# Stick-breaking attention summed by parts: the running product weighs differences of neighbouring values

## The chip, the cores and the metric

The kernel runs on one core of a Trainium2 chip. The metric is the time of one execution on the device in microseconds (us). Engines are named as in the profile: PE is TensorE (PEld its weight loads), DVE is VectorE, ACT is ScalarE, POOL is GpSimd, SP is SyncE, whose queue issues nearly all DMAs.

## The reference

Two layers of a decoder trunk for 2048 tokens of width 1024. The even layer norms, projects and runs two mixers side by side: stick-breaking attention with 8 heads of 128, and a diagonal complex SSM. Both are gated, then projected out and added to the input. The odd layer is chunked gated linear attention. The change is in the attention, which computes per head, with scores z = q k / sqrt(128) and only keys s before the query t:

```python
log_beta = jax.nn.log_sigmoid(z)
log_one_minus = jnp.where(causal, log_beta - z, 0.0)
rest = lax.cumsum(log_one_minus, axis=3, reverse=True) - log_one_minus
w = jnp.where(causal, jnp.exp(log_beta + rest), 0.0)
outs.append(jnp.einsum('bhts,bshd->bthd', w, vf[:, :kend]))
```

So the weight of key s is beta(s), the sigmoid of the score, times the product of 1 - beta over all keys between s and the query. With p(s) for the product of 1 - beta(j) over j from s up to the query, the weight of s is p(s+1) - p(s).

## The kernel before, in words

Products in single precision are made of three TensorE products each: every operand is split into a high part of 12 bits and the low rest, and `mm3` (lines 67 to 69) adds high x high, high x low and low x high in PSUM. A split is a ScalarE copy (the high part) and a subtraction on VectorE or GpSimd (the low part).

`attention` loops over the heads `h`, over macro tiles `m` of 512 tokens, and in these over two pairs `pr` of 128-query blocks.

- *Projections of a macro tile* (lines 704 to 733): four times, for 128 tokens each, the normed input is split (lines 711, 712), q, k and v of the head are formed together in `pp` (line 715), squares of q and k are summed (line 719), and GpSimd forms the reciprocal root (`qkms`, `qkrs`, lines 54 and 56). VectorE applies it (`qn`, line 725), TensorE transposes q and k (line 728), and they are split (lines 731, 732). v goes straight from PSUM into its high and low part `vhi`, `vlo` (lines 721, 722). The parts of k and v stay for the whole head in a pool of 5 (`at_kv`).
- *Attention of a pair* (lines 736 to 786): for key tiles `c` of 512 from `m` down to 0, and for each of the two query blocks: scores in PSUM (line 753; in the last tile a mask of -1e30 is added by a small product, line 756); 1 - beta as a sigmoid of -z on ScalarE (`om`, line 760); beta as a sigmoid of z on ScalarE (`be`, line 762); a scan on VectorE that multiplies 1 - beta from the last key to the first and starts from the scan of the key tile before (`pt`, line 764); beta times the running product on GpSimd (line 768); transposes of the result by TensorE into `w` (line 771); a split of it into `th`, `tl` (lines 773, 774). Then `av`, one PSUM bank, collects v times weights (line 782) over all key tiles. At the end the pair is gated with `zs` (line 785) and stored (line 786).

The weights of a head's projection come ahead of it (`AttnProj.load`, lines 654 to 665): eight loads into a pool of three buffers, each split by ScalarE and GpSimd (`whi`, `wlo`, lines 314 and 315) into a pool of eight, so that the next head's parts can be formed as the last projection of this head gives up buffers. In the last head `after(m)` also calls loads and splits for the output projection (lines 1264 to 1277); some of its products run within the end of attention.

Engines run their queues in order. Which instruction comes when in a queue is laid out at the build: the program is handed over in the order of the loops, and the scheduler orders the ready instructions by a simulated timeline with its own costs (`schedule_with_timeline_sim=True`, line 1343). It lets the projections of the next macro tile, and of the next head's first, run between the products of the attention.

Of the kernel before, what the change touches and what calls it, by code (L numbers as in the profile page):

```python
# [9 lines left out]
F32 = mybir.dt.float32  # L10
# [7 lines left out]
P = 128  # L18
# [31 lines left out]
def rsqrt_mean(e, pool, ss, n, dim, tag):  # L50
    """1 / sqrt(ss / dim + EPS) for a [P, n] tile of sums of squares."""
    nc = e.nc
    ms = pool.tile([P, n], F32, tag=tag + "ms", name=tag + "ms")
    nc.gpsimd.tensor_scalar(ms, ss, 1.0 / dim, EPS, ALU.mult, ALU.add)
    rs = pool.tile([P, n], F32, tag=tag + "rs", name=tag + "rs")
    nc.gpsimd.tensor_tensor(rs, ms, e.mhalf[:, :n], ALU.pow)
    return rs


def behind(e, i, first):  # L60
    """i comes behind first in their engine's queue"""
    e.tc.add_manual_dep(i.ins, first.ins.name, mybir.DependencyInfo(
        mybir.DependencyClass.NoSync, mybir.DependencyReason.DATA), reason="order")
# [8 lines left out]
class Norm:  # L72
    """hT[m][p, k, t] = rms_norm(x)[m * 512 + t, k * 128 + p], a token tile at a time"""
# [48 lines left out]
def s5_angles(e, s, lam_re, lam_im, log_dt):  # L122
    """lam, dt and sines of the angle of lam_bar and of its half; partitions and columns as in s5_setup"""
# [32 lines left out]
def s5_setup(e, room, lr, li, dt, sn, sh, b_re, b_im, c_re, c_im, dsk, bin_d, k0_d, co_d):  # L156
    """Chunk matrices of the SSM (8 tokens a chunk) into DRAM, powers of lam_bar into e.pw.

    Partition q = (parity, n) of pair i holds state n of group 2 * i + parity.
    bin_d[ri, i, (j, p), q] = lam_bar^(7-j) b_bar;  co_d[ri, i, q, (t, p)] = c lam_bar^(t+1)  # L160
    k0_d[g, (j, pi), (t, po)] = Re(c lam_bar^(t-j) b_bar) + d [t == j, pi == po]
    """
# [3 lines left out]
    # lam_bar^8, ^16, ^32, ^64: real parts, and (-im, im)  # L166
    e.pwr = [e.cst.tile([P, NI], F32, name=f"pwr{a}") for a in range(4)]
    e.pwi = [e.cst.tile([P, 2, NI], F32, name=f"pwi{a}") for a in range(4)]
    with e.pool("s5s", 1, "right") as s, e.pool("s5t", 2, "right") as s2, e.pool("s5w", 1, "right") as sw, \
# [41 lines left out]
        # powers  # L211
# [13 lines left out]
        def cmul(outs, xr, xi, yr, yi, sub, E):  # L225
            """outs[0] = xr yr + sub * xi yi, outs[1] = xr yi - sub * xi yr, x small, broadcast"""
            t = [s.tile([P, NI, 16], F32, tag=f"cm{a}", name=f"cm{a}") for a in range(4)]
            E.tensor_tensor(t[0], yr, bc(xr), MU)
            E.tensor_tensor(t[1], yi, bc(xi), MU)
            E.tensor_tensor(t[2], yi, bc(xr), MU)  # L230
            E.tensor_tensor(t[3], yr, bc(xi), MU)
            E.tensor_tensor(outs[0], t[0], t[1], SU if sub < 0 else AD)
            E.tensor_tensor(outs[1], t[2], t[3], AD if sub < 0 else SU)
# [17 lines left out]
        # G[tau] = c lam_bar^tau: real part, and minus the imaginary part  # L251
# [23 lines left out]
        # four groups at a time, on the partitions from 0, 32, 64 and 96  # L275
# [22 lines left out]
        # onto 16 partitions, then each row block of the chunk matrix  # L298
# [13 lines left out]
def split(nc, hi, lo, src, lo_eng):  # L312
    """hi + lo == src, each of 12 significant bits"""
    a = nc.scalar.activation(hi, src, AF.Copy)  # L314
    b = lo_eng.tensor_tensor(lo, src, hi.bitcast(F32), ALU.subtract)  # L315
    if TRACE is not None:
        TRACE.append(b)
    return a, b


# order in which a panel's last macro tile takes the weights: from low addresses on
# [3 lines left out]
class Panels:  # L325
    """Pools for weight panels of up to 512 columns, and for splits of hT."""
# [45 lines left out]
# token tiles to norm after these products (half, column block, row block)  # L372
# [3 lines left out]
def first_gates(e, pn, nrm, hT, w, c0, out_d, setup):  # L376
    """The first macro tile of gates(), as its tokens and weights come; returns the weights, and setup()."""
# [42 lines left out]
def gates(e, pn, hT, w, c0, out_d, row0, lo_eng, between=None, also=None, ws=None, sp=None, last=LAST):  # L420
    """out_d[row0 + f, t] = silu(h w[:, c0 + f]) for 512 columns; between(m) is called before macro tile m
    and gives the weights (the first tile is done), also(m, splits of hT) in it"""
# [3 lines left out]
    for m in range(4):  # L426
        if between is not None:
            if m == 0:
                continue
            ws = between(m)  # L430
        if m or sp is None:
            sp = pn.split(hT[m], lo_eng)
        pss = [pn.ps.tile([P, 512], F32, tag="ps", name="gps") for f in range(4)]
        # weights come, and are given up, one by one in the first and the last macro tile
        order = [(f, k) for f in range(4) for k in range(KD)]
        if m in (0, 3):
            order = [(f, k) for k in (range(KD) if m == 0 else last) for f in range(4)]
        for f, k in order:
            wh, wl = ws[k]
            hi, lo = sp[k // 2]  # L440
            c = slice(f * P, f * P + P)
            i = mm3(nc, pss[f], wh[:, c], wl[:, c], hi[:, k % 2], lo[:, k % 2], k == 0,
                    k == (last[-1] if m == 3 else KD - 1))
        if also is not None:
            also(m, sp, i)
        out = silu_out(e, pn, pss, m, out_d, row0)
# [3 lines left out]
def cplx_acc(e, tp, dst, src, lv, n, eng):  # L450
    """dst += lam^lv src for [P, 2, I, n] (re, im) views"""
# [13 lines left out]
def s5_in(e, pn, hT, w_in, bin_d, u_d, H, lo_eng):  # L465
    """u, and the states after the chunks, H[i // 8][:, ri, i % 8, 1 + c]"""
# [43 lines left out]
def scan_up(e, H, i1, tp, t2):  # L510
    """H[:, ri, i, 1 + c], of the 8 pairs from i1: contributions of chunks to the states after chunks 7, 15, .."""
# [24 lines left out]
def scan_down(e, H, i1, tp):  # L536
    """and to the states after all other chunks"""
# [11 lines left out]
def s5_out(e, H, u_d, k0_d, co_d, y_d):  # L549
    """y_d[ch, j, c] = gelu(ssm output) of token 8 * c + j"""  # L550
# [37 lines left out]
class Glu:  # L588
    """Weights, and all of the ssm output."""
# [23 lines left out]
def s5_glu(e, gl, m, zs_d, o_d):  # L613
    """o_d[1024 + f] = y sigmoid(y w_glu + b_glu) silu(z_b), features on rows, of 256 tokens"""
# [25 lines left out]
class AttnProj:  # L640
    """Pools for the projections of attention's heads."""
# [26 lines left out]
def attention(e, hT, w_in, zsT, oT, ap, w0, after):  # L668
    """oT[h * 128 + d, t]: gated attention; after(m) is called after the last head's projections"""
    nc, tc = e.nc, e.tc  # L670
    scale = float(DH) ** -0.5
    with ExitStack() as st:
# [13 lines left out]
        wk = pool("at_wk", 3)  # L686
# [5 lines left out]
        for h in range(HEADS):  # L692
            ws = w0 if h == 0 else ap.load(e, w_in, h)
            K, V = [], []
            for m in range(4):
# [7 lines left out]
                V.append((vhi, vlo))  # L703
                for half in range(2):
                    tp = tps.tile([P, 2, 256], F32, tag="tp", name="tp")
                    for tt in range(2):
# [14 lines left out]
                        nc.scalar.activation(vhi[:, i, :], ps[:, 2, :], AF.Copy)  # L721
                        nc.vector.tensor_tensor(vlo[:, i, :], ps[:, 2, :], vhi[:, i, :].bitcast(F32), ALU.subtract)
# [7 lines left out]
                    for j, (a, b) in enumerate(((qhi, qlo), (khi, klo))):  # L730
                        nc.scalar.activation(a[:, c0:c0 + 256], tp[:, j, :], AF.Copy)
                        nc.vector.tensor_tensor(b[:, c0:c0 + 256], tp[:, j, :], a[:, c0:c0 + 256].bitcast(F32),
                                                ALU.subtract)
                if h == HEADS - 1:
                    after(m)
                for pr in (2 * m, 2 * m + 1):
# [4 lines left out]
                    for c in range(m, -1, -1):  # L741
# [5 lines left out]
                        for i in range(2):  # L747
                            # keys of the pair's second block lie after all of its first block's queries
# [12 lines left out]
                            be = wk.tile([P, 512], F32, tag="be", name="be")  # L761
                            nc.scalar.activation(be[:, :n], z[:, :n], AF.Sigmoid, scale=scale)
# [5 lines left out]
                            nc.gpsimd.tensor_tensor(be[:, :n], be[:, :n], pt[:, lo + 1:513], ALU.mult)  # L768
                            w = wps.tile([P, 4, P], F32, tag="w", name="w")
                            for s in range(ni):  # L770
                                nc.tensor.transpose(w[:, s, :], be[:, s * P:(s + 1) * P], e.ident)  # L771
# [13 lines left out]
                    nc.vector.tensor_tensor(ot, av, zs, ALU.mult)  # L785
# [3 lines left out]
class OutW:  # L789
    """Operands of an output projection, the first weights on the right."""  # L790
# [6 lines left out]
    def fetch(self, room):  # L797
        """the next 4 rows of weights as they are, into a free tile of 16 KB"""
# [9 lines left out]
    def part(self, t, k4):  # L808
        """tile t of tokens, rows of weights from k4 * 512"""
# [9 lines left out]
    def queue(self, ab):  # L819
        """a pair of instructions, of ACT and DVE, comes behind another"""  # L820
# [9 lines left out]
    def load(self, ks, room=None):  # L830
        """splits rows ks, into the newest pool or a free tile of 16 KB"""
# [27 lines left out]
def out_proj(e, x, ow, dst_d, hT, g):  # L859
    """dst_d = x + o w, o_d with features on rows; with hT: rms_norm of it, transposed"""  # L860
    nc, ws, nk = e.nc, ow.ws, ow.nk
    with ExitStack() as st:
# [4 lines left out]
        # in banks that the phase before gives up first, away from those that the phase after begins with  # L867
# [17 lines left out]
        # the first two tiles together, at the pace at which weights come  # L885
# [11 lines left out]
        for t in range(NT):  # L897
            r0 = t * P
            if t == NT - 2 and hT is not None:
                # the last two tiles together, giving up weights from low addresses on  # L900
# [48 lines left out]
class Gla:  # L949
    """Gated linear attention: constants, the gate's code of every token, and weights ahead."""  # L950

    def __init__(self, e, hT, w_in, w_gate, b_gate, og):
# [6 lines left out]
        # the gate's code comes in 2 parts of 16 rows that add up; rows of high, low, high halves of  # L959
        # them go with rows of high, high, low halves of the weights  # L960
# [19 lines left out]
    def consts(self):  # L980
# [8 lines left out]
        # rows: key s, columns: query t, of two chunks of 64  # L989
# [18 lines left out]
    def code(self, m, sp, prev):  # L1008
        """rT: the code's part of high parts of weights, and its part of low ones, in halves"""
# [33 lines left out]
def gla(gl, zs_d, o_d, w0, after):  # L1043
    """o_d[f, t]: gated linear attention of normed, gated heads; after(m) is called after the last head's projections"""
# [6 lines left out]
    with ExitStack() as st:  # L1051
# [8 lines left out]
        def decays(h, m, va=None, vd=None):  # L1060
            """exp of the sums of log a in chunks, its inverse, and exp of what is left in the chunk"""
# [144 lines left out]
def tile_trunk(ctx, tc, x, even_norm_g, even_w_in, sb_q_norm_g, sb_k_norm_g, s5_lambda_re, s5_lambda_im, s5_log_dt,  # L1206
# [72 lines left out]
    attention(e, hT, w0, zs_d, o_d, ap, aw, after_head)  # L1279
# [67 lines left out]
```

## Time and profile before

| | |
|---|---|
| median of 3 runs | 2914.29 us (2914.11 to 2915.76) |
| profiled execution, first to last instruction (span) | 2920.8 us |
| PE, PEld busy | 2795.6, 2508.1 us |
| DVE, ACT, POOL busy | 1766.5, 1476.4, 1446.3 us |
| attention, about 590 to 1755 us of the span | 1165 us |
| mean granted clock of TensorE | 0.986 |

The profiled execution is one of its own. Its page gives the span and no other time; the span is 6.5 us above the median of the timed runs. Busy time of an engine is the time in which an instruction of it was running. In the rows of a group stand the line, the engine, the operation, the tile written and the tiles read, the count, then the busy time and the mean of one in ns, and behind the second bar the idle time of the engine just before these instructions with what ended it. In rows of waits stand who waited for whom, the us in total, the times, and the longest. In rows of a timeline stand the start, the duration, and the instruction; in rows of the chain, the start, the length and what ended last. Matmuls are pipelined: the rows of PE overlap one another.

### The profile page before, as it was taken

The numbers are of one execution on the slowest core, as the hardware profiler recorded it, in microseconds if no ns is written. First come the engines' busy times: TensorE is split into PE (matmuls) and PEld (weight loads), VectorE is DVE, ScalarE is ACT, GpSimd is POOL, SyncE is SP. The second block draws the span as 40 slices with busy tenths as digits, with TensorE's granted clock in tenths as the row PEclk, the third lists the DMA queues.
The fourth block names the chain that finished last, engine by engine and source line by source line (L and its number), as shares of the span: only waits on it lengthen the run. The fifth ranks groups of instructions, "written<-read, shape, count | busy, mean of one in ns | idle before, by whom it ended". The sixth has DMA issues, their size and how long they took to land.

```text
span 2920.8 us, 46867 instructions
## 1 busy us (share of the span) xinstructions
PE 2795.6 (96%) x17433; PEld 2508.1 (86%) x17433; DVE 1766.5 (60%) x2789; ACT 1476.4 (51%) x3244; POOL 1446.3 (50%) x1513
## 2 busy tenths in 40 slices
PE   7989979899999999999999989999999999999999
PEld 6788767898989898989898978888788999999887
DVE  7768965757686767676767674223344556565521
ACT  5475224556666656665656663222345556555310
POOL 7102821478787878787878752000023465555300
PEclk9999989999999999999999999999999999999999
DMA  5532136411010101010102114333131111121343
GB/s 167 153 79 79 58 103 216 142 30 33 19 33 19 33 19 33 22 34 19 33 19 65 48 44 141 105 104 93 58 101 37 37 59 55 41 73 62 115 142 112
DMA packets 217011, 207.17 MB, mean 71 GB/s; under 512 B 24528, under 2 KB 185712, under 8 KB 216272
## 3 DMA queue, kind: packets, MB, share of 16 engines
q1 hardware_dynamic: 216208, 202.08, 22.5%
q8 instruction: 138, 2.26, 0.3%
q10 hardware_dynamic: 576, 2.10, 0.2%
q14 instruction: 89, 0.73, 0.1%
HBM read 129.29 MB, written 74.58 MB: 70 GB/s over the span
## 4 chain that ended last, share of the span: by engine, by line
PE 73%; DVE 8%; POOL 8%; issue 5%; ACT 3%; DMA 3%; SPq 1%; POOLq 0%; ACTq 0%; DVEq 0%
PE av L782 5%; PE pp L68 5%; PE pp L67 5%; PE ops L68 5%; PE pp L69 5%; PE ops L67 5%; PE ops L69 5%; PE gps L67 4%; PE gps L68 3%; PE gps L69 3%; PE w L771 3%; DVE pt L764 2%; PE qk L67 2%; PE qk L69 2%; PE qk L68 2%
## 5 line engine op out<-in xcount | busy, mean ns | idle before, releaser
L768 POOL TENSOR_TENSOR be<-be,pt 128x512 f32<-128x512 f32 (+2 forms) x320 | 359.1, 1128 | 162.5 <-DVE pt L764 87.5
L712 POOL TENSOR_TENSOR sl<-hT,sh 128x1024 fp32r<-128x1024 f32 x128 | 331.6, 2591 | 65.0 <-ACT sh L711 64.0
L68 PE MATMUL pp<-wlo,sh 128*128 128x384 f32 x1024 | 353.0, 345 | 8.0 <-POOL wlo L315 8.0
L67 PE MATMUL pp<-whi,sh 128*128 128x384 f32 x1024 | 356.8, 349 | 2.3 <-ACT whi L314 2.3
L69 PE MATMUL pp<-whi,sl 128*128 128x384 f32 x1024 | 348.4, 340 | 0.0
L764 DVE TENSOR_TENSOR_SCAN pt<-om,pt,zero 128x513 f32<-128x513 f32 x192 | 318.7, 1660 | 19.6 <-ACT om L760 12.5
L67 PE MATMUL gps<-sh,whi 128*128 128x512 f32 (+1 forms) x672 | 253.2, 390 | 24.0 <-DVE sg L365 20.7
L68 PE MATMUL gps<-sl,whi 128*128 128x512 f32 (+1 forms) x672 | 259.3, 387 | 3.4 <-DVE sl L315 3.3
L69 PE MATMUL gps<-sh,wlo 128*128 128x512 f32 (+1 forms) x672 | 257.0, 385 | 0.0
L773 ACT ACTIVATE th<-w 128x512 fp32r<-128x512 f32 (+2 forms) x320 | 171.9, 542 | 114.1 <-PE w L771 113.0
L774 DVE TENSOR_TENSOR tl<-w,th 128x512 fp32r<-128x512 f32 (+2 forms) x320 | 187.3, 597 | 66.2 <-ACT th L773 64.7
L760 ACT ACTIVATE om<-z 128x512 f32<-128x512 f32 (+2 forms) x320 | 174.5, 545 | 104.2 <-PE z L69 75.5
L68 PEld LDWEIGHTS pp<-wlo,sh 128*128 128x128 f32 x1024 | 193.7, 189 | 18.1 <-POOL wlo L315 15.6
L315 DVE TENSOR_TENSOR sl<-hT,sh 128x1024 fp32r<-128x1024 f32 (+1 forms) x148 | 173.0, 1192 | 51.0 <-ACT sh L314 49.0
L67 PEld LDWEIGHTS pp<-whi,sh 128*128 128x128 f32 x1024 | 195.0, 190 | 8.2 <-ACT whi L314 5.4
L69 PE MATMUL ops<-woh,ol 128*128 128x512 f32 x496 | 196.7, 397 | 0.0
L68 PE MATMUL ops<-wol,oh 128*128 128x512 f32 x496 | 196.3, 396 | 0.0
L67 PE MATMUL ops<-woh,oh 128*128 128x512 f32 x496 | 195.6, 395 | 0.0
L69 PEld LDWEIGHTS pp<-whi,sl 128*128 128x128 f32 x1024 | 193.0, 189 | 2.4
L314 ACT ACTIVATE sh<-hT 128x1024 fp32r<-128x1024 f32 (+1 forms) x148 | 155.6, 1090 | 61.6 <-PE gps L69 32.6
L711 ACT ACTIVATE sh<-hT 128x1024 fp32r<-128x1024 f32 x128 | 135.9, 1062 | 97.7 <-PE pp L68 97.1
L771 PE MATMUL w<-ident,be 128*128 128x128 f32 x1088 | 170.7, 274 | 8.5 <-POOL be L768 5.8
(326 smaller groups left out, 8249.2 us busy)
## 6 DMA issues: line engine op xcount, KB each, us to landing
zs_d<-sg SPq DMA_DIRECT2D x80, 256.0 KB
o<-o_d SPq DMA_DIRECT2D x80, 256.0 KB
xt<-in_x_dram SPq DMA_DIRECT2D x28, 512.0 KB
r<-in_even_w_in_dram SPq DMA_DIRECT2D x64, 192.0 KB
zs<-zs_d SPq DMA_DIRECT2D x64, 128.0 KB
o_d<-ot SPq DMA_DIRECT2D x64, 128.0 KB
r<-in_odd_w_in_dram SPq DMA_DIRECT2D x64, 128.0 KB
zs<-zs_d SPq DMA_DIRECT2D x32, 256.0 KB
```

Of the source, the lines that this page charges most:

```text
L67: nc.tensor.matmul(out, lhsT=lhi, rhs=rhi, start=start, stop=False)
L68: nc.tensor.matmul(out, lhsT=lhi, rhs=rlo, start=False, stop=False)
L69: return nc.tensor.matmul(out, lhsT=llo, rhs=rhi, start=False, stop=stop)
L314: a = nc.scalar.activation(hi, src, AF.Copy)
L315: b = lo_eng.tensor_tensor(lo, src, hi.bitcast(F32), ALU.subtract)
L712: nc.gpsimd.tensor_tensor(sl, ht, sh.bitcast(F32), ALU.subtract)
L760: nc.scalar.activation(o[:, lo:512], z[:, :n], AF.Sigmoid, scale=-scale)
L764: nc.vector.tensor_tensor_scan(pt[:, lo:][:, ::-1], o[:, lo:][:, ::-1], zr.to_broadcast([P, n + 1]), 1.0 if prev[i] is None else prev[i], ...
L768: nc.gpsimd.tensor_tensor(be[:, :n], be[:, :n], pt[:, lo + 1:513], ALU.mult)
L771: nc.tensor.transpose(w[:, s, :], be[:, s * P:(s + 1) * P], e.ident)
L773: nc.scalar.activation(th[:, :ni, qs], w[:, :ni, :], AF.Copy)
L774: nc.vector.tensor_tensor(tl[:, :ni, qs], w[:, :ni, :], th[:, :ni, qs].bitcast(F32), ALU.subtract)
```

## The change

With p as above, the sum over keys of (p(s+1) - p(s)) v(s) is rearranged by parts: for a query t it is the sum over s of p(s) (v(s-1) - v(s)), plus the value of the last key. Masked keys have 1 - beta = 1, so the kernel may run the sum to the end of the query's 128-block, and what is added is the last v of that block.

- The sigmoid for beta (line 762) and GpSimd's product (line 768) go. The transposes (line 771) read the scan `pt` itself. The pool that held `be` and `pt` in 3 buffers each holds `pt` in 4.
- v is first copied whole into `vf` (128x4x128, a new pool of 2). Per macro tile, `dv` is `vf` moved on by one token: one DMA of 127 rows, one row for the blocks' first tokens, and one row from the macro tile before (for the first, a memset on GpSimd). GpSimd subtracts `vf` from `dv`, and the difference is split into `vhi`, `vlo` for the whole macro tile at once, ScalarE for the high and GpSimd for the low part. The four low parts on VectorE per macro tile (line 722) go.
- The last v of each of the four blocks is written to a DRAM tile `ve_d` and read back transposed into `ve` (128x4).
- The gating (line 785) becomes two instructions of 128 columns for one of 256: (av + ve) * zs.

The diff, without lines in which only comments go:

```diff
@@ attention
-def attention(e, hT, w_in, zsT, oT, ap, w0, after):
+def attention(e, hT, w_in, zsT, oT, ve_d, ap, w0, after):
...
-        wk = pool("at_wk", 3)
+        vp = pool("at_v", 2)
+        wk = pool("at_wk", 4)
...
+                vf = vp.tile([P, 4, P], F32, tag="vf", name="vf")
...
-                        nc.scalar.activation(vhi[:, i, :], ps[:, 2, :], AF.Copy)
-                        nc.vector.tensor_tensor(vlo[:, i, :], ps[:, 2, :], vhi[:, i, :].bitcast(F32), ALU.subtract)
+                        nc.scalar.activation(vf[:, i, :], ps[:, 2, :], AF.Copy)
...
+                dv = vp.tile([P, 4, P], F32, tag="dv", name="dv")
+                ve = vp.tile([P, 4], F32, tag="ve", name="ve")
+                if m == 0:
+                    nc.gpsimd.memset(dv[0:1, 0, :], 0.0)
+                else:
+                    nc.sync.dma_start(out=dv[0:1, 0, :], in_=vl[P - 1:P, 3, :])
+                nc.sync.dma_start(out=dv[1:P], in_=vf[0:P - 1])
+                nc.sync.dma_start(out=dv[0:1, 1:4, :], in_=vf[P - 1:P, 0:3, :])
+                nc.sync.dma_start(out=ve_d[h:h + 1, m * 4:m * 4 + 4], in_=vf[P - 1:P])
+                nc.sync.dma_start(out=ve, in_=ve_d[h, m * 4:m * 4 + 4].rearrange("i d -> d i"))
+                nc.gpsimd.tensor_tensor(dv, dv, vf, ALU.subtract)
+                split(nc, vhi, vlo, dv, nc.gpsimd)
+                vl = vf
...
-                            be = wk.tile([P, 512], F32, tag="be", name="be")
-                            nc.scalar.activation(be[:, :n], z[:, :n], AF.Sigmoid, scale=scale)
...
-                            nc.gpsimd.tensor_tensor(be[:, :n], be[:, :n], pt[:, lo + 1:513], ALU.mult)
...
-                                nc.tensor.transpose(w[:, s, :], be[:, s * P:(s + 1) * P], e.ident)
+                                nc.tensor.transpose(w[:, s, :], pt[:, lo + s * P:lo + (s + 1) * P], e.ident)
...
-                    nc.vector.tensor_tensor(ot, av, zs, ALU.mult)
+                    for i in range(2):
+                        qs, b = slice(i * P, (i + 1) * P), pr % 2 * 2 + i
+                        nc.vector.scalar_tensor_tensor(ot[:, qs], av[:, qs], ve[:, b:b + 1], zs[:, qs], ALU.add, ALU.mult)
...
-    attention(e, hT, w0, zs_d, o_d, ap, aw, after_head)
+    attention(e, hT, w0, zs_d, o_d, dram("ve_d", [HEADS, NT, DH]), ap, aw, after_head)
```

## The prediction

> **What bounds the kernel now.** First the page: the span, the busy shares, TensorE's slices, the chain that ended last.
>
> ```profile
> span 2920.8 us, 46867 instructions
> ...
> PE 2795.6 (96%) x17433; PEld 2508.1 (86%) x17433; DVE 1766.5 (60%) x2789; ACT 1476.4 (51%) x3244; POOL 1446.3 (50%) x1513
> ...
> PE   7989979899999999999999989999999999999999
> ...
> PE 73%; DVE 8%; POOL 8%; issue 5%; ACT 3%; DMA 3%; SPq 1%; POOLq 0%; ACTq 0%; DVEq 0%
> ```
>
> TensorE is busy 96% of the span and carries 73% of the chain. A slice is 73 us; attention runs from about 590 to 1755 us, slices 8 to 23, at "9" but for the last, with "8". The change takes work from ScalarE, GpSimd and VectorE and none from TensorE, so only the time in which TensorE stands still there can be won. The second view, stages of attention: the first head, the next two, the five steady ones, the tail behind the last projections.
>
> ```profile
> core 0: us, PE busy (x) PEld busy (x) DVE busy (x) ACT busy (x) POOL busy (x), PEclk, DMA share, GB/s
> 590.00:730.00 140.00, 132.37 (x824) 123.42 (x824) 95.90 (x140) 80.19 (x221) 108.06 (x94) 0.99 0.09 27
> 730.00:980.00 250.00, 244.95 (x1594) 231.05 (x1593) 179.92 (x267) 158.14 (x423) 196.74 (x163) 1.00 0.08 23
> 980.00:1690.00 710.00, 695.25 (x4482) 647.55 (x4480) 492.94 (x754) 450.00 (x1191) 580.78 (x480) 1.00 0.11 33
> 1690.00:1755.00 65.00, 56.99 (x345) 49.06 (x346) 53.28 (x67) 41.68 (x83) 34.71 (x31) 0.97 0.20 58
> sum 1165.00, PE 1129.57 PEld 1051.08 DVE 822.03 ACT 730.01 POOL 920.29; mean PE 282.39 PEld 262.77 DVE 205.51 ACT 182.50 POOL 230.07
> ```
>
> TensorE stands still for 7.6, 5.1, 14.8 and 8.0 us: 35.4 us of 1165. That is the most that removing other engines' work can free there, apart from the clock (below). The third view, who ended TensorE's waits in that stretch:
>
> ```profile
> PE tp L728 <- DVE qn L725: 10.8, 12, 3.3
> PE pp L68 <- POOL wlo L315: 8.0, 10, 1.1
> PE w L771 <- POOL be L768: 5.8, 16, 1.0
> ...
> PE pp L67 <- ACT whi L314: 2.3, 5, 0.6
> PE av L782 <- ACT be L762: 1.5, 1, 1.5
> ```
>
> Transposes of normed queries and loads of weights meet where one head's projections end and the next head's begin. There the timeline shows GpSimd's queue:
>
> ```profile
> 1119.98 2.01 POOL L768 TENSOR_TENSOR be<-be,pt 128x512 f32<-128x512 f32 x1
> 1122.07 0.19 POOL L54 TENSOR_SCALAR qkms<-ss 128x2 f32<-128x2 f32 x1
> ...
> 1123.32 0.70 POOL L56 TENSOR_TENSOR qkrs<-qkms,mhalf 128x2 f32<-128x2 f32 x1
> 1123.98 1.09 POOL L768 TENSOR_TENSOR be<-be,pt 128x512 f32<-128x512 f32 x1
> ...
> 1124.46 0.33 PE L728 MATMUL tp<-ident,qn 128*128 128x128 f32 x1 [0.55 <-DVE qn L725]
> ```
>
> The beta product of 2.01 us sits in front of the two small instructions that the normed queries wait for; TensorE waits behind them.
>
> **The change, part by part.** Durations:
>
> ```profile
> L768 POOL TENSOR_TENSOR be<-be,pt 128x512 f32<-128x512 f32 (+2 forms) x320 | 359.1, 1128 | 162.5 <-DVE pt L764 87.5 <-PE tp L728 17.0 <-ACT be L762 13.1
> ...
> L764 DVE TENSOR_TENSOR_SCAN pt<-om,pt,zero 128x513 f32<-128x513 f32 x192 | 318.7, 1660 | 19.6 <-ACT om L760 12.5 <-POOL be L768 2.6
> ...
> L762 ACT ACTIVATE be<-z 128x512 f32<-128x512 f32 (+2 forms) x320 | 174.7, 546 | 0.0
> ...
> L725 DVE SCALAR_TENSOR_TENSOR qn<-pp,qkrs,gqk 128x128 f32<-128x128 f32 x254 | 77.2, 346 | 165.1 <-POOL qkrs L56 165.0
> ...
> L722 DVE TENSOR_TENSOR vlo<-pp,vhi 128x128 fp32r<-128x128 f32 x127 | 35.9, 283 | 29.7 <-ACT vhi L721 29.5
> ```
>
> ```profile
> L785 DVE TENSOR_TENSOR ot<-av,zs x64: 392/414/427, 610.5 to 1750.6; 128x256 f32<-128x256 f32 x64
> ```
>
> *Removed.* 320 sigmoids on ScalarE (174.7 us) and 320 products on GpSimd (359.1 us), both between scores and weights: the transposes now follow the scan itself. VectorE loses 127 low parts of v (35.9 us). *Added.* Per head and 512 keys, 32 times: two GpSimd subtractions and one ScalarE copy of 128x512, 4 or 5 DMAs, and on VectorE four gating instructions of 128x128 for two of 128x256. A lone 128x512 on GpSimd took 1.09 us, a disturbed one 2.01 (both shown), so GpSimd gets back 70 to 129 us and is 230 to 289 lighter. ScalarE gets back 32 x 0.55 = 17, so 157 lighter. VectorE gets 128 x 0.346 - 64 x 0.414 = 17.8 back, so 18 lighter. The scans should gain too:
>
> ```profile
> 812.26 2.39 POOL L712 TENSOR_TENSOR sl<-hT,sh 128x1024 fp32r<-128x1024 f32 x1
> 812.36 3.37 DVE L764 TENSOR_TENSOR_SCAN pt<-om,pt,zero 128x513 f32<-128x513 f32 x1 [0.28 <-ACT om L760]
> ...
> 1742.61 1.27 DVE L764 TENSOR_TENSOR_SCAN pt<-om,pt,zero 128x513 f32<-128x513 f32 x1
> ```
>
> Beside a GpSimd subtraction the scan took 3.37 us, alone 1.27; the mean is 1.66. Less GpSimd work pulls it towards 1.27. TensorE's products and transposes stay as many and as large.
>
> What TensorE gets of this, by its waits:
> - Waits of transposes for the product, 5.8 us (longest 1.0): the scan ends a product's 1.09 us earlier, more than the longest of them. All 5.8 go. The 1.5 us put down to the beta sigmoid go as well. Together 7.3 (bounds 4 and 7.3).
> - Waits for normed queries, 10.8 us: the product is out of the queue, but square, mean and root remain. I take 7 (bounds 3 and 10.8).
> - Waits for weights' low parts, 8.0 us: behind the products, but also behind loads. I take half, 4 (bounds 0 and 8).
> - The remaining 9.3 us (35.4 less the above): products of the tail that wait for their weights, and small ones. Each unit of the tail is shorter by product and sigmoid, 1.09 + 0.55. I take 2 (bounds 0 and 9.3).
> - The clock. After the longest waits it is lower for a while:
>
> ```profile
> 723.92 0.59 PE L728 MATMUL tp<-ident,qn 128*128 128x128 f32 x2 [3.30 <-DVE qn L725]
> ```
>
> ```profile
> 724.68 0.18 PE pp L68
> ...
> 725.71 0.32 PE pp L67
> ```
>
> ```profile
> 1700.00:1710.00 10.00, 7.59 (x37) 6.40 (x38) 7.96 (x12) 5.05 (x13) 7.04 (x8) 0.83 0.33 103
> ```
>
> A granted clock of 0.83 over 10 us is 3.4 us at half, which loses 1.7; the steps of 0.32 for 0.18 show the other such place, just behind the longest wait for normed queries (3.30). I take 2 of the 3.4 (bounds 0 and 3.4).
>
> Gain: 7.3 + 7 + 4 + 2 + 2 = 22 us; bounds 7 and 38.8 (35.4 + 3.4).
>
> What it may cost: v used to be ready 0.28 us after its copy; now there is a chain. Three DMAs must be issued and must land, then GpSimd subtracts, ScalarE copies, GpSimd subtracts. The trace has a DMA inside the on-chip memory, one of 512 single numbers like the read of `ve`, and the slack:
>
> ```profile
> 144.73 2.96 DMA ka<-kt
> ...
> 155.78 2.02 DMA ka<-kt
> ```
>
> ```profile
> L609 SPq DMA_DIRECT2D bg<-in_s_b_glu_dram x1: 383/383/383, 523.3 to 523.3; - x1
> ```
>
> ```profile
> 1131.86 0.28 ACT L721 ACTIVATE vhi<-pp 128x128 fp32r<-128x128 f32 x1
> ```
>
> ```profile
> 1141.10 0.34 PE L782 MATMUL av<-th,vhi 128*128 128x256 f32 x2
> ```
>
> Issue 3 x 0.38, landing 2.02 to 2.96, subtractions 1.09 to 2.01 each, copy 0.55: 5.9 to 8.7 us. Slack: this block's last v copy ends at 1132.14 and the first product with it starts at 1141.10, 9.0 us later, the shortest of the 32 such stretches. The weights' side is to become 1.6 us quicker, which leaves 7.3. So the chain is hidden at its low end and 1.4 us late at its high end. `ve` goes through DRAM and back, two landings in series, 4 to 6 us; it is needed at the gating, a whole pair of query blocks later, and that covers it.
>
> The Trainium skill speaks against this read: its page "DMA: Bandwidth & Descriptors", section "Rules for kernel authors", says that a last dimension that isn't contiguous becomes one descriptor per element and should be rearranged. The trace agrees only in part: the DMA of this kind held the queue for 0.383 us, and its landing is not shown. By that rule a landing of some us more would still lie under the pair of query blocks, and the sum stays.
>
> Queues: behind a GpSimd subtraction that waits for its DMA stand the splits for the next projections and the roots; behind ScalarE's copy, the sigmoids; on SP, the loads of the next weights behind the new DMAs, or these behind a load that waits for room:
>
> ```profile
> SPq L660 <- POOL wlo L315: 121.6, 53, 7.9
> ```
>
> ```profile
> ACT whi L314 <- DMA r<-in_even_w_in_dram: 32.6, 14, 3.6
> ```
>
> The nearest row for such a blocked queue is the last one: ScalarE stood 32.6 us for late loads, and TensorE then waited 2.3 us for its high parts, 7%, or 10.3 (32%) with the low parts counted in. With 64 new waiting points of about 1 us, 7% is 4.5. I take 5 (bounds 0 and 64 x 1 x 0.32 = 20, more if the chain itself is late). The order within the queues is planned anew at the build; the trace of before can't show it, and these bounds have to hold it.
>
> Sum: -22 + 5 = -17 us. The profiled execution has a span of 2920.8, 6.5 above the runs' median of 2914.3; I put the difference on the median: 2897 us.
>
> **The rivals.**
> 1. *All standing goes.* With GpSimd 25 to 31% lighter (230 to 289 of 920 us) no queue is late, no wait is new: -38.8, so 2875.5. For it: 24.6 of the 28.4 us of waits shown end on GpSimd or on what waits for it. Against: loads from DRAM pace the weights too.
> 2. *Nothing to measure.* Weights are paced by loads and their three buffers, normed queries by their own chain; only the 7.3 us go and 5 come back: 2912. For it: the 121.6 us of SP waiting for room. Against: the 2.01 us product ahead of the root.
> 3. *Slower: v's chain ends last.* Blocks 1 to 3 of each head, 24 in all, have the short slack. With a split of 2.39 us ahead of the subtraction the chain is 5.9 + 2.39 = 8.3 to 11.1 us against 7.3, 1.0 to 3.8 late, and TensorE, in order, stands at the first product. At 1.5 late: 24 x 1.5 - 22 = +14, so 2928. From 22/24 = 0.9 us per block it is a loss, from 1.2 a measurable one. Against: between blocks TensorE has projections to do, if they stand ahead of that product in its order.
>
> On the third: the steps of 0.32 above show what a wait of 3.3 us cost in clock. The Trainium skill, "TensorE: Matmul & The Clock Gate", section "What's actually happening", says that the clock falls to half after an idle window of about 3.4 us; by it, stalls of 1.5 us would add nothing, while stalls of 3.8 us would add 1.7 each. The trace agrees with the half, but shows it after waits shorter than that window.
>
> That the change would not do what it says is excluded: both lines are deleted.
>
> **How the numbers follow.** A measurement tells about 0.2% (5.8 us) from no change. Forecast (6 to 28 us faster) 0.50, rival 1 (more) 0.12, rival 2 (within 5.8) 0.18, rival 3 (slower) 0.20. So faster 0.62, same 0.18, slower 0.20. The bounds of the terms give 2875.5 (38.8 and no cost) to 2927 (7 and 20). The range goes from 2877, which leaves out the last of rival 1, to 2930, which takes in rival 3 up to a loss of 16 us: about 0.15 is outside. The forecast's own range is 2886 to 2908.
>
> **What would show it.** In the profile after: GpSimd about 260 us less busy and ScalarE about 157; TensorE's busy time in attention still 1130; its waits for normed queries about 4 us, for weights about 4, none for the product; scans nearer 1.4 us; attention about 17 us shorter, half of that before 980 us and in the tail; no new granted clock below 1. Wrong would be waits of TensorE for v's parts or of GpSimd for the new DMAs that come back as TensorE's waits (rival 3), or unchanged waits for weights (rival 2).

## The result, and the profile after

The changed kernel takes 3215.48 us (median of 4 runs, 3213.06 to 3220.49) against 2914.25 us for the kernel before beside it (4 runs, 2914.11 to 2915.76): 1.1031 of its time, 95% interval 1.1016 to 1.1047. It is 301.2 us slower. The forecast was 2897 us with a range of 2877 to 2930: wrong in sign, and outside the range.

The page of the changed kernel: span, busy shares, TensorE's slices with the granted clock under them, and the chain that ended last.

```profile
span 3218.8 us, 46191 instructions
...
PE 2862.0 (89%) x17433; PEld 2577.8 (80%) x17433; DVE 1739.6 (54%) x2725; ACT 1357.6 (42%) x2956; POOL 1177.6 (37%) x1265
...
PE   7899799877788788878788788999999999999999
...
PEclk9999899888898898889898898999999999999999
...
PE 64%; DMA 16%; DVE 6%; POOL 5%; ACT 4%; issue 4%; SPq 1%; POOLq 0%; ACTq 0%; DVEq 0%
DMA dv<-vf 9%; PE av L799 5%; PE ops L67 4%; PE ops L68 4%; PE ops L69 4%; PE pp L68 3%; PE pp L67 3%; PE pp L69 3%; DMA ve_d<-vf 3%; PE w L788 3%; PE gps L67 3%; PE gps L68 3%; PE gps L69 3%; PE qk L67 2%; PE qk L69 2%
```

GpSimd and ScalarE are lighter, as the diff says, and the products of TensorE are as many as before (17433). But from slice 7 to 24, the first being 0, TensorE is at "7" and "8", where it was at "9", the clock under it at 0.8 to 0.9, and DMAs hold 16% of the chain for 3%. One of them leads the list by line: `dv<-vf`, the move of v by one row.

Stages next: attention of the kernel before as one stretch, with the same count of TensorE's instructions as the kernel after,

```profile
590.00:1752.00 1162.00, 1126.57 (x7226) 1048.64 (x7227) 819.03 (x1225) 727.01 (x1915) 917.29 (x765) 1.00 0.10 31
```

and of the kernel after, followed by seven microseconds inside it (the last three columns: granted clock, busy share of the 16 DMA engines, GB/s).

```profile
590.00:2053.00 1463.00, 1193.64 (x7226) 1118.49 (x7227) 793.81 (x1164) 609.05 (x1633) 649.26 (x516) 0.88 0.11 30
...
1337.00:1344.00 7.00, 5.82 (x40) 5.50 (x38) 0.00 (x0) 0.00 (x0) 0.00 (x0) 1.00 0.07 25
```

Attention went from 1162 to 1463 us: +301, all of the loss. TensorE's standing time went from 35.4 to 269.4 us (+234). Its busy time rose by 67 us for the same instructions, at a mean granted clock of 0.88 for 1.00.

Who waited for whom in that stretch of the kernel after (us in total, times, longest):

```profile
POOL dv L751 <- DMA dv<-vf: 297.4, 30, 10.7
...
ACT vhi L314 <- POOL dv L751: 269.3, 25, 14.1
...
PE av L799 <- ACT th L790: 115.2, 19, 7.6
...
PE z L67 <- ACT om L780: 73.9, 7, 10.8
...
PE av L799 <- ACT vhi L314: 48.1, 7, 6.9
...
ACT whi L314 <- DMA r<-in_even_w_in_dram: 120.3, 19, 14.0
```

TensorE waits for ScalarE for 237.2 us (115.2 + 73.9 + 48.1), and the timeline shows two ways to it. In most macro tiles three queues stand in line: GpSimd for the DMA, ScalarE for GpSimd, TensorE for ScalarE. Of TensorE's 163.3 us there (115.2 + 48.1), the larger part is for `th`, which has nothing to do with v: it stood behind the v copy in ScalarE's queue. The timeline of one such macro tile, rows of SP, GpSimd, ScalarE and TensorE:

```profile
1331.28 0.63 SPq L747 DMA_DIRECT2D dv<-vf  x1
1331.96 4.12 SPq L749 DMA_DIRECT2D ve_d<-vf  x1
...
1338.10 0.28 PE L799 MATMUL av<-th,vlo 128*128 128x256 f32 x1
...
1344.97 1.26 POOL L751 TENSOR_TENSOR dv<-dv,vf 128x512 f32<-128x512 f32 x1 [10.63 <-DMA dv<-vf]
...
1346.27 0.63 ACT L314 ACTIVATE vhi<-dv 128x512 fp32r<-128x512 f32 x1 [12.36 <-POOL dv L751]
1346.81 1.04 ACT L718 ACTIVATE sh<-hT 128x1024 fp32r<-128x1024 f32 x1
...
1348.41 0.60 ACT L790 ACTIVATE th<-w 128x512 fp32r<-128x512 f32 x1
...
1349.07 0.58 PE L799 MATMUL av<-th,vhi 128*128 128x256 f32 x1 [6.24 <-ACT th L790]
```

The DMA is issued at 1331.28 and lands at 1344.81, 13.53 us later by the chain of waits:

```profile
1331.28 13.53 DMA dv<-vf
```

ScalarE idles 12.36 us at `vhi`, and only then comes to `th`. TensorE had work for about half of that time and idles 6.24 us. The first product behind takes 0.58 us where the last one before took 0.28.

The 73.9 us for `om`, seven waits of 10.2 to 10.9 us, have another way. They stand where a head ends, in front of the v copy, behind a copy of the next head's weights. One of them, rows of SP, ScalarE and TensorE:

```profile
732.06 0.66 SPq L747 DMA_DIRECT2D dv<-vf  x1
...
746.14 0.38 SPq L750 DMA_DIRECT2D ve<-ve_d  x1
746.62 2.01 SPq L660 DMA_DIRECT2D r<-in_even_w_in_dram  x3
...
749.30 0.52 ACT L314 ACTIVATE whi<-r 128x384 fp32r<-128x384 f32 x1 [13.91 <-DMA r<-in_even_w_in_dram]
...
750.36 0.80 PE L67 MATMUL z<-khi,qhi 128*128 128x512 f32 x1 [10.85 <-ACT om L780]
```

SP reads `ve` back only when its write, queued behind the 127 rows, has landed, and issues the next load of weights after that. ScalarE idles 13.91 us for the load, with `om` behind it.

### The profile page after: what moved, and what is told of

Same layout as the page of the kernel before. It is cut to its first block, busy times and chain, and to the rows that moved or that the text cites. A ratio compares the mean times of both kernels' runs of the same rounds, so it can differ in the third digit from the quotient of the medians.

```text
span 3218.8 us, 46191 instructions
## 1 busy us (share of the span) xinstructions
PE 2862.0 (89%) x17433; PEld 2577.8 (80%) x17433; DVE 1739.6 (54%) x2725; ACT 1357.6 (42%) x2956; POOL 1177.6 (37%) x1265
## 4 chain that ended last, share of the span: by engine, by line
PE 64%; DMA 16%; DVE 6%; POOL 5%; ACT 4%; issue 4%; SPq 1%; POOLq 0%; ACTq 0%; DVEq 0%
DMA dv<-vf 9%; PE av L799 5%; PE ops L67 4%; PE ops L68 4%; PE ops L69 4%; PE pp L68 3%; PE pp L67 3%; PE pp L69 3%; DMA ve_d<-vf 3%; PE w L788 3%; PE gps L67 3%; PE gps L68 3%; PE gps L69 3%; PE qk L67 2%; PE qk L69 2%
## 5 line engine op out<-in xcount | busy, mean ns | idle before, releaser
L67 PE MATMUL pp<-whi,sh 128*128 128x384 f32 x1024 | 363.8, 355 | 0.0
L69 PE MATMUL pp<-whi,sl 128*128 128x384 f32 x1024 | 358.2, 350 | 0.0
L799 PE MATMUL av<-th,vhi 128*128 128x256 f32 x576 | 160.0, 297 | 167.5 <-ACT th L790 115.2
L799 PEld LDWEIGHTS av<-th,vhi 128*128 128x128 f32 x576 | 115.3, 205 | 176.6 <-ACT th L790 121.3
L790 ACT ACTIVATE th<-w 128x512 fp32r<-128x512 f32 (+2 forms) x320 | 164.2, 535 | 181.9 <-PE w L788 181.1
L68 PEld LDWEIGHTS pp<-wlo,sh 128*128 128x128 f32 x1024 | 202.3, 198 | 2.4
L788 PE MATMUL w<-ident,pt 128*128 128x128 f32 x1088 | 183.8, 294 | 22.2 <-DVE pt L782 13.1
L67 PE MATMUL z<-khi,qhi 128*128 128x512 f32 (+2 forms) x320 | 136.7, 434 | 74.4 <-ACT om L780 73.9
L69 PEld LDWEIGHTS pp<-whi,sl 128*128 128x128 f32 x1024 | 199.7, 195 | 3.1
L780 ACT ACTIVATE om<-z 128x512 f32<-128x512 f32 (+2 forms) x320 | 167.8, 537 | 80.9 <-PE z L69 39.5
```

Source lines behind the costliest of these rows:

```text
L67: nc.tensor.matmul(out, lhsT=lhi, rhs=rhi, start=start, stop=False)
L68: nc.tensor.matmul(out, lhsT=lhi, rhs=rlo, start=False, stop=False)
L69: return nc.tensor.matmul(out, lhsT=llo, rhs=rhi, start=False, stop=stop)
L780: nc.scalar.activation(o[:, lo:512], z[:, :n], AF.Sigmoid, scale=-scale)
L788: nc.tensor.transpose(w[:, s, :], pt[:, lo + s * P:lo + (s + 1) * P], e.ident)
L790: nc.scalar.activation(th[:, :ni, qs], w[:, :ni, :], AF.Copy)
```

## Experiments

A "before" beside a time is the kernel before on the same chip, 7 runs each. The unchanged lines of the changed kernel stand in all of them.

### Does the move's landing carry the loss? Move and last value, apart and together

First the row count of the one large DMA: 127 rows as 112 and 15.

```diff
-nc.sync.dma_start(out=dv[1:P], in_=vf[0:P - 1])
+nc.sync.dma_start(out=dv[1:113], in_=vf[0:112])
+nc.sync.dma_start(out=dv[113:P], in_=vf[112:P - 1])
```

> The DMA of 127 rows is issued as two, of 112 and of 15 rows; all else as in the change. Theory 'one engine': the move of 127 rows is slow by itself (13.5 us from issue to landing in the profile after, at 22 to 27 GB/s), because a count of rows that has no divisor up to 16 is carried by a single DMA engine; 112 and 15 rows are spread. Then the landing falls to 2 to 4 us, GpSimd's waits for dv from 297 us to under 60, and the time to 2900 to 2960 us. Theory 'SP queue': what holds is SP, which stands 265 us for the write of ve_d before it reads it back, with loads and stores behind; then that wait stays and the time stays above 3100. Theory 'order': the queues' new order loses by itself; then dv lands early, the waits move elsewhere, and the time stays above 3000.

Measured: 2880.66 us (4 runs, 2878.05 to 2882.18) against 2918.64 before: ratio 0.9872, interval 0.9856 to 0.9888. One more DMA of the same bytes makes a kernel that is 10% slower into one that is 1.3% faster, faster than the 2900 to 2960 us of the theory that it bears out. Its attention, waits, the issue of the 112 rows on SP and the chain:

```profile
590.00:1714.00 1124.00, 1103.63 (x7229) 1042.86 (x7230) 809.40 (x1164) 611.66 (x1633) 681.14 (x516) 1.00 0.14 39
```

```profile
ACT vhi L314 <- POOL dv L752: 22.2, 15, 4.1
...
PE w L789 <- DVE pt L783: 8.1, 16, 2.0
...
PE tp L734 <- DVE qn L731: 5.7, 1, 5.7
...
PE av L800 <- POOL vlo L315: 5.0, 7, 0.7
...
POOL dv L752 <- DMA dv<-vf: 1.3, 1, 1.3
```

```profile
1044.39 0.53 SPq L747 DMA_DIRECT2D dv<-vf  x1
...
1044.97 2.22 DMA dv<-vf
```

The chain's row starts with the last DMA that `dv` waits for, here that of 15 rows. From the issue of the large DMA until all of `dv` has landed (called landing from here on) it is 2.8 us for 13.5, in other macro tiles up to 3.5. GpSimd's wait for it 1.3 us for 297.4, ScalarE's 22.2 for 269.3, and the granted clock in attention 1.00.

Then, with the 127 rows kept, the other new path taken out: no last value through DRAM.

```diff
-nc.sync.dma_start(out=ve_d[h:h + 1, m * 4:m * 4 + 4], in_=vf[P - 1:P])
-nc.sync.dma_start(out=ve, in_=ve_d[h, m * 4:m * 4 + 4].rearrange("i d -> d i"))
+nc.gpsimd.memset(ve, 0.0)
```

> Leaves out the last values of the blocks: ve is set to zero by GpSimd, and neither the write to DRAM nor the read back is issued. The DMA of 127 rows stays. Theory 'one engine': GpSimd still waits some 10 us for dv in each of the 32 macro tiles, time above 3130. Theory 'SP queue': 265 us of SP's waiting go and most of the loss with them, time under 3000.

Measured: 3198.2 us in one run, before 2918.64. Of 301 us the last value carries about 17 (3215.5 less 3198.2, two chips), although the chain of the kernel after puts 3% of its share on `ve_d<-vf` and SP waits long there. The 17 us are found again in TensorE's waits for `om`, 73.9 us with the last value and 17.7 less without:

```profile
PE z L67 <- ACT om L779: 56.2, 7, 8.1
```

The weights' loads no longer stand behind the read of `ve`. They still land late beside the 127 rows (one 11.2 us after its issue), so most of these waits stay.

Then the move taken out, with and without the last value.

```diff
-if m == 0:
-    nc.gpsimd.memset(dv[0:1, 0, :], 0.0)
-else:
-    nc.sync.dma_start(out=dv[0:1, 0, :], in_=vl[P - 1:P, 3, :])
-nc.sync.dma_start(out=dv[1:P], in_=vf[0:P - 1])
-nc.sync.dma_start(out=dv[0:1, 1:4, :], in_=vf[P - 1:P, 0:3, :])
-nc.gpsimd.tensor_tensor(dv, dv, vf, ALU.subtract)
+nc.gpsimd.tensor_tensor(dv, vf, vf, ALU.add)
```

> Leaves out the move by one token: the three DMAs into dv and the memset go, dv is formed by GpSimd from vf alone (vf + vf) in an instruction of the same size. ve stays with its write and read. Theory 'one engine': the loss is gone, 2890 to 2940, and SP's waits for ve_d fall to about 2.5 us each (80 us), since the write no longer stands behind the 127 rows. Theory 'SP queue': SP still waits for each ve_d, time above 3050. Theory 'order': above 3000.

> Leaves out both, the move by one token and the last values: what stays of the change is its arithmetic and the work it removes. This is the gain term of the prediction alone: 22 us less than before, bounds 7 and 39, so 2892 (2875 to 2907). If the queues' new order loses by itself, it is above 2914.

Measured: 2883.02 us without the move (one run), 2888.37 us without either (4 runs, 2885.46 to 2889.99; ratio 0.9896, interval 0.9877 to 0.9915), both beside 2918.64. With the move in 112 and 15 rows the kernel is no slower than with no move at all, so a landing of 2.8 to 3.5 us costs nothing that can be measured. The version with less to do is 8 us slower than the one with all of it. The likeliest reason is the order, laid out anew at each build, which no run holds fixed; differences under about 8 us between versions are taken here to say nothing about a cause.

### Is it the landing, and by what rule? Row counts in between

122 and 5 rows, then 124 and 3:

```diff
+nc.sync.dma_start(out=dv[1:123], in_=vf[0:122])
+nc.sync.dma_start(out=dv[123:P], in_=vf[122:P - 1])
```

```diff
+nc.sync.dma_start(out=dv[1:125], in_=vf[0:124])
+nc.sync.dma_start(out=dv[125:P], in_=vf[124:P - 1])
```

> The 127 rows go as 122 and 5. Theory 'one engine' in its exact form: the rows are dealt to as many DMA engines as the largest divisor up to 16; 122 = 2 x 61 gives two engines. From 13.5 us for 127 rows on one and about 2.4 us for 112 + 15 (16 and 15 engines) a row takes some 0.09 us, so 61 rows in turn land after about 7.4 us. Rival: 127 is slow for being odd or prime, and an even count is as quick as 112: 2.4 us. For the time: if every us of landing costs in each of 32 macro tiles, 2880 + 32 x 5 = 3040; if the slack in front of the first product swallows part of it, 2940 to 3000.

> The 127 rows go as 124 and 3. By the same rule 124 = 4 x 31 gives four engines and a landing of about 4.7 us. For the time: if every us costs, 2880 + 32 x 2.3 = 2954; if there is slack, 2880 to 2910.

Measured, one run each, before 2918.85: 2996.21 us with 122 rows, 2927.16 us with 124, the second between the two times expected. SP's issue, the chain and the waits of the 122 rows,

```profile
606.49 0.71 SPq L747 DMA_DIRECT2D dv<-vf  x1
...
607.25 7.33 DMA dv<-vf
```

```profile
POOL dv L752 <- DMA dv<-vf: 141.7, 31, 6.1
```

a stretch inside one of its moves,

```profile
608.00:613.00 5.00, 5.00 (x32) 4.96 (x31) 2.03 (x5) 1.74 (x6) 1.46 (x3) 1.00 0.14 40
```

and of the 124 rows, where the chain's row starts with the large DMA itself:

```profile
604.42 6.14 DMA dv<-vf
```

```profile
POOL dv L752 <- DMA dv<-vf: 85.4, 31, 4.1
```

```profile
607.50:609.50 2.00, 2.00 (x15) 1.97 (x14) 0.61 (x2) 1.26 (x4) 0.04 (x1) 1.00 0.24 81
```

All move about the same 254 KB. In the stretches quoted the DMA engines are busy by 0.07 with 127 rows, by 0.14 with 122 and by 0.24 with 124: one sixteenth is 0.0625, two are 0.125, four are 0.25. 127 has no divisor up to 16 but 1, 122 has 2, 124 has 4, 112 has 16, and the landings go that way, though not in proportion: 13.5, 8.1, 6.1 and 2.8 us in the rows shown. That 127 is slow for being odd is excluded, since 122 and 124 are slow too. The Trainium skill says this outright: "DMA: Bandwidth & Descriptors", section "Why a DMA increments its semaphore by 16 and not by 1", takes as the number of DMA engines the largest divisor up to 16 that both sides' outermost counts share, and gives 127 partitions as its example of one engine. The trace agrees. The 122 and the 124 rows landed later than expected (7.4 and 4.7 us): the expectations took 2.4 us for the 112 rows, a length that starts at the issue of the 15 rows.

| large DMA, rows | landing, us | GpSimd's wait, us | clock in attention | time, us |
|---|---|---|---|---|
| 112 | 2.8 to 3.5 | 1.3 | 1.00 | 2880.66 |
| 124 (one run) | 6.1 to 7.2 | 85.4 | 0.99 | 2927.16 |
| 122 (one run) | 8.0 to 8.7 | 141.7 | 0.96 | 2996.21 |
| 127 | 13.5 to 13.6 | 297.4 | 0.88 | 3215.48 |

Against the first line, 84.1 us of GpSimd's wait cost 46.5 us, 140.4 cost 115.6, and 296.1 cost 334.8: 0.55, 0.82 and 1.13 us per us. Queues swallow the first part; at the end the clock and the late weights add to it.

### What is the gain made of, with the landing out of the way?

The version with 112 rows gains 38 us, more than the forecast. One engine at a time gets its load back, in results that nobody reads: GpSimd a product per unit, after the scan,

```diff
+bx = wx.tile([P, 512], F32, tag="bx", name="bx")
+nc.gpsimd.tensor_tensor(bx[:, :n], o[:, lo:512], pt[:, lo + 1:513], ALU.mult)
```

or ScalarE a second sigmoid, both on top of the 112 and 15 rows.

```diff
+bx = wx.tile([P, 512], F32, tag="bx", name="bx")
+nc.scalar.activation(bx[:, :n], z[:, :n], AF.Sigmoid, scale=scale)
```

> The rows go as 112 and 15, and GpSimd forms a product of the old size for every unit again (of 1 - beta and the running product, into a tile that nobody reads), right behind the scan. ScalarE's second sigmoid stays out and the transposes still read the scan. Theory 'load': the gain of 38 us over before comes from GpSimd's queue, so most of it is lost: 2905 to 2920. Theory 'chain': it comes from the shorter way from scores to weights, so the unread product costs little: 2880 to 2890.

> The rows go as 112 and 15, and ScalarE forms the second sigmoid again for every unit, into a tile that nobody reads. GpSimd's product stays out. Theory 'load' for ScalarE: 175 us more on ScalarE, right behind the first sigmoid, put back some of the gain: 2890 to 2905. Theory 'ScalarE is free': 2878 to 2885.

Measured, before 2918.85: 2963.28 us with the product (4 runs, 2961.07 to 2965.24; ratio 1.0153, interval 1.0136 to 1.017), 2874.53 us with the sigmoid (4 runs, 2871.56 to 2879.99; ratio 0.9854, interval 0.9836 to 0.9871). The product costs more than either theory had, and ScalarE's load costs nothing: attention with 736.73 us of it, more than before the change, is 9 us shorter than with 611.66.

```profile
590.00:1705.00 1115.00, 1103.68 (x7224) 1040.11 (x7225) 762.54 (x1164) 736.73 (x1952) 631.85 (x513) 1.00 0.14 39
```

The price of GpSimd's product is not clean. It also reads `om` and holds that tile until GpSimd has come round, and ScalarE waits for the room:

```profile
ACT om L782 <- POOL bx L789: 71.8, 55, 3.6
```

So once more with a product that reads only the scan's result:

```diff
-nc.gpsimd.tensor_tensor(bx[:, :n], o[:, lo:512], pt[:, lo + 1:513], ALU.mult)
+nc.gpsimd.tensor_tensor(bx[:, :n], pt[:, lo:512], pt[:, lo + 1:513], ALU.mult)
```

> As the run in which GpSimd forms an unread product again, but that product reads the running product alone (itself moved by one column) and so no longer holds the tile of 1 - beta, for which ScalarE stood 71.8 us in 55 waits there. If the 83 us lost in that run were GpSimd's load, the time stays at 2940 to 2965; if they came mostly of the held tile, it falls to 2890 to 2925.

Measured: 2934.52 us (4 runs, 2931.45 to 2935.94), before 2917.73; ratio 1.0052, interval 1.0037 to 1.0067. That is between the two times expected: of the 83 us that the first product cost, about 29 were the held tile and about 54 come with GpSimd's load. Its attention and TensorE's waits:

```profile
590.00:1766.00 1176.00, 1122.75 (x7225) 1042.87 (x7226) 863.90 (x1163) 623.71 (x1628) 1029.32 (x833) 0.99 0.13 37
```

```profile
PE w L792 <- DVE tl L795: 18.9, 28, 1.9
PE tp L735 <- DVE qn L732: 11.5, 8, 5.6
PE av L803 <- DVE ot L808: 9.9, 7, 1.4
PE av L803 <- ACT th L794: 9.8, 10, 1.4
```

Against the version with 112 rows GpSimd does 348 us more (1029.3 for 681.1) and attention is 52 us longer, 0.15 us per us. By that price the 236 us that the change takes from GpSimd (917.3 to 681.1) are worth 35 us of the 38. The proportion is an assumption, since the load put back is larger than the load taken away. TensorE's waits now end mostly on VectorE, which is also 54 us busier (863.9 for 809.4) with no work added: its scans are longer. First the scans of this version, then those of the version with 112 rows:

```profile
L784 DVE TENSOR_TENSOR_SCAN pt<-om,pt,zero 128x513 f32<-128x513 f32 x192 | 341.5, 1789 | 10.6 <-ACT om L782 6.3 <-POOL bx L789 3.4
...
L784 DVE TENSOR_TENSOR_SCAN pt<-om,zero 128x129 f32<-128x129 f32 (+3 forms) x128 | 196.7, 1564 | 17.2 <-ACT om L782 17.1
```

```profile
L783 DVE TENSOR_TENSOR_SCAN pt<-om,pt,zero 128x513 f32<-128x513 f32 x192 | 328.2, 1720 | 25.3 <-ACT om L781 24.7 <-PE w L789 0.2
...
L783 DVE TENSOR_TENSOR_SCAN pt<-om,zero 128x129 f32<-128x129 f32 (+3 forms) x128 | 152.7, 1218 | 60.1 <-ACT om L781 60.1
```

Whether the 54 us come through GpSimd's queue, with normed queries late behind it, or through scans slowed by 57 us beside it, these runs don't separate.

Last, the load moved the other way: VectorE takes the low part of v's difference, then the subtraction too.

```diff
-split(nc, vhi, vlo, dv, nc.gpsimd)
+split(nc, vhi, vlo, dv, nc.vector)
```

```diff
-nc.gpsimd.tensor_tensor(dv, dv, vf, ALU.subtract)
+nc.vector.tensor_tensor(dv, dv, vf, ALU.subtract)
```

> 112 and 15 rows, and the low part of the differences is formed on VectorE instead of GpSimd, which took 1.57 us for each of 32 there, and behind which TensorE stood 5.0 us. VectorE should take about 0.7 us, so the way to v is 0.9 us shorter, but VectorE, 72% busy in attention, gets 22 us more. Expected: 2870 to 2885, that is about as fast as with 112 and 15 rows alone (2880.7).

> 112 and 15 rows, and both the subtraction of neighbouring values and the low part on VectorE. GpSimd is 92 us lighter than with 112 and 15 rows alone, VectorE 45 us heavier, the way to v 1.5 us shorter. If GpSimd's queue still decides, 2865 to 2880; if VectorE's does, for which TensorE's transposes wait 8 us now, 2885 to 2895.

Measured, before 2917.73: 2877.02 us with the first edit (4 runs, 2872.05 to 2879.16; ratio 0.9851, interval 0.9833 to 0.9869) and 2873.02 us with both (4 runs, 2871.92 to 2874.24; ratio 0.9843, interval 0.9828 to 0.9858).

```profile
590.00:1707.00 1117.00, 1101.99 (x7224) 1044.42 (x7225) 818.19 (x1228) 606.78 (x1632) 575.83 (x452) 1.00 0.14 40
```

Both beat the kernel before; the last, whose row stands above, has the lowest time of all versions, with 15.0 us of TensorE's standing left (1117.0 less 1102.0). Their intervals overlap with that of the 112 rows, so the move to VectorE itself is not shown to gain.

## Why the prediction was wrong, step by step

**The step that failed: the landing.** The prediction took "landing 2.02 to 2.96" for the new DMA from the two rows `DMA ka<-kt`, the nearest move inside the on-chip memory. In the code that DMA (lines 302 and 303) has 16 rows outermost, and the new one 127. The place was near, the bytes were not (32 KB for 254), but they are not what was missed: 254 KB as 112 and 15 rows landed in 2.8 to 3.5 us. The count that decides was not looked at. Measured: 13.5 us, one DMA engine, 25 GB/s. The prediction's chain of 5.9 to 8.7 us becomes 17.4 to 19.3 with it.

**Rival 3 was the right mechanism, at a price far too low.** "v's chain ends last" is what happened in most macro tiles. Its 2928 came from being 1.5 us late. With the landing as measured, its own sum is 10.1 to 12.0 us late (chain less its slack of 7.3); over the 30 waits for the DMA, 30 x 10.1 - 22 = 281 and 30 x 12.0 - 22 = 338 stand around the measured 301. That is in part chance. TensorE's waits on this way were 7.6 us at most, the longer ones came by the late weights, and 67 us of the 301 are the clock, which is not in the sum. With 124 rows, landing after 6.1 to 6.3 us in most macro tiles, the same sum gives 58 to 120 us of loss; measured were 8 (2927.16 beside 2918.85). The slack was too short: 9.0 us was rightly the shortest stretch, but counted by the products of `av` in the trace of before, the 24 stretches that were said to have it have a median of 11.4. So the point of decision, 1.2 us late, was set too early.

**Queues.** The prediction named ScalarE's copy and "behind ScalarE's copy, the sigmoids", and priced a blocked queue at 7% to 32% of its wait. With a landing of 2.8 to 3.5 us that holds: ScalarE waits 22.2 us, and the new waits of TensorE for v's low parts are 5.0, where 5 was taken. With 13.5 us, 163.3 of ScalarE's 269.3 us come through, 61%. A share taken from waits of 3.6 us at most was used where the wait could be 14. It also named "on SP, the loads of the next weights behind the new DMAs": that is the way of the 73.9 us for `om`, and it had no term of its own.

**The clock.** "No new granted clock below 1" was wrong: 0.88, and 67 us of busy time for the same instructions. The prediction's sentence from the Trainium skill ("TensorE: Matmul & The Clock Gate", "What's actually happening"), that idling past some 3.4 us brings half the clock, agrees here: after 6.24 us of idling a product took 0.58 us, 0.28 before, and a stall of 6 to 11 us came in nearly every macro tile. In the version with 112 rows attention shows 1.00.

**What of the gain held.** The version with 112 rows is the change as it was forecast, and shows the terms.
- The net of standing was right: 35.4 to 20.4 us, -15.0, where -20 and 5 of cost were summed (22 less 2 for the clock).
- Its parts were not all right. The 7.3 us for the product came back as 8.1 us of waits for the scan: the transposes wait for the next slowest. Of the 10.8 us for normed queries 5.7 remain, in one wait. Those for weights' low parts went, all 8.0.
- "That is the most that removing other engines' work can free" was wrong. TensorE's busy time fell too, 1126.57 to 1103.63 us for as many products, where 1130 was to stay. So of the 38 us by which attention got shorter, 23 came out of time that counted as busy, and a bound made of standing time was none. Why the same products were busy for less is not shown. The weight loads, in the column behind, tell it better: they were busy 1048.64 of 1162 us, so without a load for 113.4, and 1042.86 of 1124, so 81.1: 32 of the 38 us. The Trainium skill, "Perfetto Trace Analysis", section "Identifying the Most-Contended Engine", says that the busy share of matmuls is no good measure of the distance to the bound since they are pipelined, and puts the share of peak arithmetic and that of weight loads in its place; the trace agrees as far as the two shares go.
- GpSimd 236 us lighter in attention (230 to 289 forecast). ScalarE 115 (157 forecast): instructions one behind the other overlap, in the timeline above the copy `sh` starts at 1346.81 while `vhi` runs to 1346.90, so a group's sum of durations is more than the busy time that goes with it. The second sigmoid, put back, tells the same: 178.1 us by its row, 125.1 us of busy time. VectorE 10 (18 and the scans forecast).

**The scans** were to come from 1.66 us towards 1.4 as GpSimd got lighter. They came to 1.72 us in the version with 112 rows (row above). With the second sigmoid, which adds nothing to GpSimd, they came to 1.45:

```profile
L786 DVE TENSOR_TENSOR_SCAN pt<-om,pt,zero 128x513 f32<-128x513 f32 x192 | 276.9, 1449 | 20.3 <-ACT om L782 19.3
```

What changed besides the sigmoid is the order, and so perhaps which GpSimd instruction runs beside which scan; that is not shown. And 51 us less of scans went with 6 us less of time. In this pair the length of the scans neither follows GpSimd's work nor sets the end.

**The last value.** "Hidden" was nearly right: some 17 us while the move held up its DMA engine, by way of the weights, and nothing to be measured in the pair of versions without the move.

## What to carry to other kernels

Before pricing a DMA by a row of the trace, compare the outermost counts: a move by one partition has 127 rows, which went over one DMA engine here, and 112 + 15 rows landed in about a quarter of the time. A late operand costs less by itself than by the in-order queue in which its copy waits: list what stands behind it, in the queue that issues the DMAs too. And standing time of a busy engine is no upper bound of what lighter neighbours can give.

## What the runs showed of the hardware beyond that

- SP's issue of the next DMA was held behind the 127 rows: there the one-row write of `ve_d` took 4.12 us to issue (above; the median of all 32 is 4.22), behind 122 rows (median 0.41) and behind 112 and 15 it was not held:

```profile
1045.88 0.41 SPq L750 DMA_DIRECT2D ve_d<-vf  x1
```

- A GpSimd instruction that holds a tile with few buffers cost about 29 us by way of the engine that refills it (ScalarE's 71.8 us of waits for `om`), over half of what its own load cost.
